# A two-layer hybrid decoder trunk: weight splits with priority, query stacks prepared earlier, selection rounds moved forward

## The chip, the cores and the metric

The kernel runs on one core of a Trainium2 chip. The core has five engines that run their own instruction queues side by side: TensorE (PE in the profile; PEld are its weight loads), VectorE (DVE), ScalarE (ACT), GpSimd (POOL) and SyncE (SP), which only issues DMAs here. The metric is the device time of one execution in microseconds; the runs of a kernel are summed up by their median.

## The reference, cut to what matters

A sequence of 512 tokens of width 1024 passes two layers. Each layer norms its input, projects it, and splits the columns among four attention groups of four heads each; their outputs are concatenated, projected and added, and a squared-ReLU MLP follows.

```
for l in range(2):
    h = rms_norm(x, norm1[l]);  proj = h @ w_in[l]            # 1024 -> 2764 columns
    # A: latent attention: q = rms_norm(a_cq) @ w_uq, k,v = rms_norm(a_ckv) @ w_ukv, rope on 32 of 96
    # B: sliding window of 128 keys, 2 key heads, a sink logit per head
    # C: score = sum_h w_h * relu(q_idx_h . k_idx); each query keeps its 128 best keys, attends over them
    # D: causal attention with a bias of cumulative log forget gates
    x = x + concat(o_a, o_b, o_c, o_d) @ w_out[l]
    x = x + square(relu(rms_norm(x, norm2[l]) @ w_up[l])) @ w_down[l]
out = rms_norm(x, final_norm)
```

All of it is float32.

## The kernel before

**Precision.** A float32 product is made of three matmuls (`mm3`, L126 to L129): each operand is split into a high part (a rounded copy, usually on ACT, L112) and a low part (what is left, a subtract, L122), and high by high, low by high and high by low are summed. So every weight tile of 128x1024 that is loaded (`raw`, three buffers, L206) goes through `split_weight` (L176): ACT writes `wh`, DVE or POOL writes `wl`. `weight` (L186) makes these splits one tile ahead of their use; letters in `PRM` (`wloi` to `wlop`) name the engine of each low part. The 16 tiles of `ww_d` in a layer hold the projection columns of groups B, C and D.

**Order.** PE's instructions stand as the code issues them. Those of the other engines are put in order by a scheduler at build time, which takes what it holds to be ready and, among these, what was issued first; `tc.high_priority(offset=HIGH)` moves what is issued under it ahead in that choice. Each engine then runs its list strictly as it stands and waits where an operand is not there.

**A layer's attention.** The projections are a `queue` of generators: `a` (32 steps of three matmuls, 416 columns), then `b0`, `b`, `d0`, `d`, `dv`, `c0`, `c`, `cv` (32 steps each, 256 columns), then the output projection's four parts. Wherever the code has work that leaves PE waiting, `fill(kind)` (L335) advances that queue by as many steps as a digit in `PLACES` says: `idx`, `qi` and `isc` in group C's indexer (`isc`: one digit for each of the 24 score products, L749), `aq` and `cq` around the transposes of the latent inputs (L816), `up` behind each tile of the latent query and key products, `a0` behind each step of the first pair's preparation.

Group A works on pairs of heads. `prep_a` turns its queries and keys by PE transposes (L491 in `parts`; L854 for the rotated 32 columns), splits them (`prt`, `kst`), and fills four stacks per pair by DMAs from SBUF to SBUF (`move`, L485, on SP's queue). The first pair's preparation is finished before the first unit.

**Units.** 64 units follow (head by query block of 128): 0 to 15 group A, 16 to 31 group B, 32 to 47 group D, 48 to 63 group C. A unit is a score on PE (L894 to L897 for A, L1003 to L1006 for B), a row maximum on DVE (`mn`, L541), the exponential on ACT (L544), the normalisation on POOL (L549), transposes on PE two units later (L555), their split, and the product with the values. `pace` puts projection steps between, so that PE gets 2600 ns of work per unit. The `softmax` and what follows on it is issued with high priority; the preparation of later families (`prep_b` and so on, with their `prt` splits and moves) and the selection are not.

**Selection.** Group C needs the 128 best of up to 512 keys per query: 16 rounds for each of three query blocks, each round a pair of DVE instructions (L770 finds the eight largest, L771 strikes them out). These 48 pairs are spread over the units by `extra` in `run_units`: `PRM["selr"]` gives the pairs per unit in units 0 to 15, 16 to 31, 32 to 47 and 48 to 63; at unit 45 all that are left are issued.

Of the kernel before, what the change touches and what calls it, by code (L numbers as in the profile page):

```python
# [16 lines left out]
P = 128  # L17
NL = 2
NT = 4
# [13 lines left out]
PLACES = {  # L33
    "idx": "k",
    "qi": "11111111",
    "isc": "111111111111111111111111",
    "cq": "444",
    "up": "22222222",
    "a0": "880",
    "aq": "606",  # L40
}

PRM = {
    "hold": ['g', 'b1'], "q3": "VGV", "high": 200, "gate_b": -1, "gate_d0": -1, "lag_b": 6, "lag_c": 4,
    "steps": 2, "pace": 2600, "quantum": 360, "burst": 5, "mlag": 4, "first": [0, 11, 18, 21, 26, 33, 41, 48], "psa": 2, "pss": 2, "pst": 3,
    "norm": "G", "vlo": "V", "wloi": "GVVV", "wloa": "VGGV",
    "wlo0": "GGVV", "wlo1": "GVGV", "wlop": "GGGG", "selr": [1.4, 1.0, 1.0, 1.2], "tlag": 2,
    "plag": 2, "rote": "VVGV", "rotp": "GVGGVGGGGVGVGGVG",
}

# [2 lines left out]
def tile_trunk(ctx: ExitStack, tc: tile.TileContext, x_d, consts_d, gains_d, sinks_d, fb_d, fin_d,  # L53
# [104 lines left out]
        return y  # L158


    wlist = []
    for L in range(NL):
        wlist += [(wi_d[L, kk], 600, WLI[kk], "y" if L and kk > 1 else "") for kk in range(4)]
        wlist += [(wa_d[L, kk], 832, WLA[kk], "") for kk in range(4)]
        wlist += [(ww_d[L, i, kk], 1024, (WL0 if i < 2 else WL1)[(2 * i + kk) % 4], "") for i in range(8) for kk in range(2)]
        for i in range(4):
            wlist += [(wo_d[L, i, :, 0:1024], 1024, WLP[i], ""), (wo_d[L, i, :, 1024:1536], 512, WLP[i], "")]
        wlist += [(wt_d[L, c], 1024, G, "") for c in range(2)]
        for half in range(2):
            wlist += [(wu_d[L, 16 * half + i], 1024, V, "") for i in range(16)]  # L170
            wlist += [(wd_d[L, half, c, fp], 1024, V, "x" if half and c and fp > 3 else "")
                      for c in range(2) for fp in range(8)]
    w_raw, w_split, w_at = [], [], [0]

    def split_weight(r, n, h, l, eng):
        hi(h, r[:, 0:n], S)  # L176
        lo(l, r[:, 0:n], h, eng)
# [7 lines left out]
    def weight(i, ahead=1):  # L185
        while len(w_raw) < min(len(wlist), i + 4) or len(w_split) < min(len(wlist), i + 1 + ahead):  # L186
            j = len(w_split)
            if j < min(len(w_raw), i + 1 + ahead):
                _, n, eng, where = wlist[j]
                p, c = (w_pools[where], 600 if where == "y" else 1024) if where else (whl, 1024)  # L190
                h = p.tile([P, c], F32R, tag="wh" + where, name="wh")
                l = p.tile([P, c], F32R, tag="wl" + where, name="wl")
                split_weight(w_raw[j], n, h[:, 0:n], l[:, 0:n], eng)
                w_split.append((h, l))
            else:
                load_weight()
        return w_split[i]
# [111 lines left out]
    for L in range(NL):  # L309
# [4 lines left out]
        with ExitStack() as ph:  # L314
# [17 lines left out]
            def ytile():  # L332
                return y_p.tile([P, NT, 256], F32, tag="y", name="y")
# [35 lines left out]
            def fill(kind):  # L369

                n = Q.get(kind, "")
                j = site.get(kind, 0)
                site[kind] = j + 1
                for _ in range(int(n[j], 36) if j < len(n) else 0):
                    if not queue or not advance():
                        break
# [435 lines left out]
            for j in range(3):  # L812
                fill("aq")
                ps = bank_b()
# [14 lines left out]
            hi(k2s[0][64:128, 0], ps[64:128], S)  # L829
            lo(k3s[64:96], ps[64:96], k2s[0][64:96, 0], V)  # L830
            ykn, ykv, yqn, yqr = (ytile() for _ in range(4))
            for t in range(NT):
                ps = bank("s")
                c = slice(t * P, (t + 1) * P)
                for j in range(2):
                    mm3(ps[:, 0:384], cth[j][:, c], ctl[j][:, c], wq_h[:, j * 384:(j + 1) * 384],
                        wq_l[:, j * 384:(j + 1) * 384], j == 0, j == 1)
                hi(yqr[:, t, 0:128], ps[:, 256:384], S, r2[:, t:t + 1])
                hi(yqn[:, t], ps[:, 0:256], S, r2[:, t:t + 1])
                rotate(yqr[:, t, 0:128], 4, 16, t, V)  # L840
                fill("up")
            for t in range(NT):
                ps = bank("s")
                c = slice(t * P, (t + 1) * P)
                mm3(ps, cth[2][:, c], ctl[2][:, c], wkv[:, 0], wkv[:, 1], True, True)
                hi(ykn[:, t], ps[:, 0:256], S, r2[:, 4 + t:5 + t])
                hi(ykv[:, t], ps[:, 256:512], S, r2[:, 4 + t:5 + t])
                fill("up")

            def prep_a(o, p):  # L850
                if p == 0:
                    ps = bank("t")
                    for t in range(NT):
                        T.transpose(ps[:, t * P:(t + 1) * P], yqr[:, t, 0:128], idf)  # L854
                    qrs.extend((kstack(), kstack()))
                    hi(qrs[0], ps, S)
                    lo(qrs[1], ps, qrs[0], V)
                if p:
                    k2s.append(stack())
                o["k1"], o["k2"], o["q1"], o["q2"] = stack(), k2s[p], stack(), stack()  # L860
                for h in range(2):
                    r = slice(64 * p + 32 * h, 64 * p + 32 * h + 32)
                    move(o["q2"][64:96, h], qrs[0][r])
                    move(o["q2"][96:128, h], qrs[1][r])
                for h in range(2):
                    if p or h:
                        move(o["k2"][64:128, h], k2s[0][64:128, 0])
                h_, l_ = parts(ykn, 128 * p)
                for h in range(2):
                    r = slice(64 * h, 64 * h + 64)  # L870
                    move(o["k1"][0:64, h], h_[r])
                    move(o["k1"][64:128, h], h_[r])
                    move(o["k2"][0:64, h], l_[r])
                yield
                h_, l_ = parts(yqn, 128 * p)
                for h in range(2):
                    r = slice(64 * h, 64 * h + 64)
                    move(o["q1"][0:64, h], h_[r])
                    move(o["q1"][64:128, h], l_[r])
                    move(o["q2"][0:64, h], h_[r])  # L880
                yield
                if p == 0:
                    o["vs"] = v_pair(heads(ykv, 0))
                    yield
# [2 lines left out]
                o["vs"] = v_pair(heads(ykv, P))  # L887
                yield

            qrs = []  # L890

            def score_a(o, ps, h, qb, n):
                c = slice(qb * P, (qb + 1) * P)
# [134 lines left out]
            units = []  # L1028
            os_ = {}
            for p in range(2):  # L1030
                o = os_["a", p] = {}
                preps.append((f"a{p}", FIRST[0], (), prep_a(o, p)))
                if p:
                    preps.append(("a1v", 8, (), prep_av(o)))
                units += causal_units(f"a{p}", score_a, o, p, lambda n: 3 * (n + 32) / 2.4 + 67)
# [301 lines left out]
```

## Time and profile before

| | |
|---|---|
| median of 3 runs | 1322.31 us (1321.92 to 1323.63) |
| the profiled execution | 1321.27 us, its span 1319.4 us |
| PE busy | 1257.7 us (95% of the span) |
| DVE busy | 758.3 us (57%) |
| ACT busy | 572.4 us (43%) |
| POOL busy | 260.3 us (20%) |
| mean granted clock of TensorE | 0.984 |

The span runs from the first to the last instruction of the profiled execution. Busy time of PE is time in which a matmul is in flight, at whatever clock; the granted clock is 1.00 at full speed (2.4 GHz) and 0.50 at half (1.2 GHz), so a window with a value between was at half speed for a part of it. The attention of the first layer takes the first 300 us or so of the span, its MLP the time to about 650 us, and the second layer repeats both.

### The profile page before, as it was taken

How to read it: one execution, taken by the hardware profiler on the slowest of the kernel's cores; microseconds unless marked ns; L12 is line 12 of the kernel's file. 1: busy time of each engine (PE TensorE's matmuls, PEld its weight loads, DVE VectorE, ACT ScalarE, POOL GpSimd, SP SyncE). 2: the span in 40 equal slices, each digit the busy share in tenths (PEclk: the TensorE clock that was granted, in tenths of full speed). 3: DMA queues.
4: the chain of work that ended last, by engine and by line, in shares of the span. 5: the costliest groups of instructions: out<-in, count | busy, mean ns of one | idle time of the engine just before them, and what ended most of it. 6: DMA issues, size and time to landing. Idle time of an engine off the chain costs nothing.

```text
span 1319.4 us, 19401 instructions
## 1 busy us (share of the span) xinstructions
PE 1257.7 (95%) x7232; PEld 1102.7 (84%) x7232; DVE 758.3 (57%) x1557; ACT 572.4 (43%) x1159; POOL 260.3 (20%) x356
## 2 busy tenths in 40 slices
PE   8798989999999999999998899899999999999997
PEld 7798878897888888888897889788988888888885
DVE  5677999845453334433366599997454523444344
ACT  5564555643442123323337455566344421233231
POOL 3353345441000000000033432454300000000011
PEclk9899989999999999999998999899999999999999
DMA  6126334523333333334411443453322333333331
GB/s 184 65 89 158 97 87 114 154 88 93 88 106 97 96 96 96 96 96 128 141 62 61 124 128 82 121 126 102 123 84 92 105 97 96 96 96 100 108 112 64
DMA packets 50818, 136.79 MB, mean 104 GB/s; under 512 B 7460, under 2 KB 7716, under 8 KB 50724
## 3 DMA queue, kind: packets, MB, share of 16 engines
q1 hardware_dynamic: 50724, 135.55, 35.6%
q8 instruction: 57, 0.93, 0.3%
q14 instruction: 37, 0.30, 0.1%
HBM read 106.95 MB, written 4.19 MB: 84 GB/s over the span
## 4 chain that ended last, share of the span: by engine, by line
PE 81%; DVE 13%; ACT 2%; DMA 1%; issue 1%; SPq 1%; POOL 1%; POOLq 0%; DVEq 0%; ACTq 0%
PE bank L129 24%; PE bank L127 24%; PE bank L128 24%; DVE isc L771 2%; DVE mn L541 2%; PE bank L555 2%; DVE m L770 2%; DVE pt1l L122 1%; DMA stk<-prt 1%; DVE wl L122 1%; PE bank L491 1%; PE bank L602 1%; PE bank L237 1%; ACT y L114 1%; PE bank L749 1%
## 5 line engine op out<-in xcount | busy, mean ns | idle before, releaser
L122 DVE TENSOR_TENSOR wl<-raw,wh 128x1024 fp32r<-128x1024 f32 (+2 forms) x154 | 186.5, 1213 | 229.7 <-ACT wh L112 229.0
L112 ACT ACTIVATE wh<-raw 128x1024 fp32r<-128x1024 f32 (+2 forms) x196 | 199.1, 1018 | 264.7 <-PE bank L128 229.2
L127 PE MATMUL bank<-wh,T 128*128 128x256 f32 (+3 forms) x864 | 272.5, 315 | 3.3 <-ACT T L241 1.8
L129 PE MATMUL bank<-wl,T 128*128 128x256 f32 (+3 forms) x864 | 257.5, 298 | 17.0 <-DVE wl L122 14.3
L128 PE MATMUL bank<-wh,T 128*128 128x256 f32 (+3 forms) x864 | 256.1, 296 | 0.2 <-DVE T L124 0.2
L129 PE MATMUL bank<-T,wh 128*128 128x512 f32 x512 | 199.5, 390 | 0.9 <-DVE T L124 0.9
L127 PE MATMUL bank<-T,wh 128*128 128x512 f32 x512 | 199.8, 390 | 0.0
L127 PE MATMUL bank<-wh,gh 128*128 128x512 f32 x512 | 199.6, 390 | 0.0
L128 PE MATMUL bank<-T,wl 128*128 128x512 f32 x512 | 199.5, 390 | 0.0
L129 PE MATMUL bank<-wl,gh 128*128 128x512 f32 x512 | 199.2, 389 | 0.0
L128 PE MATMUL bank<-wh,gl 128*128 128x512 f32 x512 | 199.2, 389 | 0.0
L129 PEld LDWEIGHTS bank<-wl,T 128*128 128x128 f32 x864 | 167.2, 194 | 20.8 <-DVE wl L122 15.2
L122 POOL TENSOR_TENSOR wl<-raw,wh 128x1024 fp32r<-128x1024 f32 (+3 forms) x42 | 91.8, 2185 | 420.7 <-DVE wl L122 336.5
L127 PEld LDWEIGHTS bank<-wh,T 128*128 128x128 f32 x864 | 168.5, 195 | 5.8 <-ACT T L241 2.2
L128 PEld LDWEIGHTS bank<-wh,T 128*128 128x128 f32 x864 | 167.9, 194 | 3.9 <-DVE T L124 0.5
L1134 DVE TENSOR_TENSOR a<-a 128x512 f32<-128x512 f32 x64 | 44.4, 693 | 154.1 <-ACT a L1133 154.1
L1133 ACT ACTIVATE a<-bank 128x512 f32<-128x512 f32 x64 | 38.3, 599 | 201.1 <-PE bank L129 201.1
L129 PEld LDWEIGHTS bank<-T,wh 128*128 128x128 f32 x512 | 96.1, 188 | 21.9 <-DVE T L124 1.8
L128 PEld LDWEIGHTS bank<-T,wl 128*128 128x128 f32 x512 | 96.1, 188 | 20.5 <-DVE wl L122 0.7
L127 PEld LDWEIGHTS bank<-T,wh 128*128 128x128 f32 x512 | 96.1, 188 | 19.9 <-ACT T L241 0.3
L129 PEld LDWEIGHTS bank<-wl,gh 128*128 128x128 f32 x512 | 96.1, 188 | 19.9
L127 PEld LDWEIGHTS bank<-wh,gh 128*128 128x128 f32 x512 | 96.1, 188 | 19.9
(223 smaller groups left out, 1847.0 us busy)
## 6 DMA issues: line engine op xcount, KB each, us to landing
raw<-in_wu_dram SPq DMA_DIRECT2D x64, 512.0 KB, 3.6
raw<-in_wd_dram SPq DMA_DIRECT2D x64, 512.0 KB, 3.6
stk<-prt SPq DMA_DIRECT2D x144, 128.0 KB, 2.4
raw<-in_ww_dram SPq DMA_DIRECT2D x32, 512.0 KB, 3.5
T<-in_x_dram SPq DMA_DIRECT2D x16, 256.0 KB, 4.2
raw<-in_wo_dram SPq DMA_DIRECT2D x8, 512.0 KB, 3.7
raw<-in_wa_dram SPq DMA_DIRECT2D x8, 416.0 KB, 3.2
raw<-in_wi_dram SPq DMA_DIRECT2D x8, 300.0 KB, 3.5
```

The source lines that it names most:

```text
L112: S.activation(out=out, in_=in_, func=AF.Copy)
L114: S.activation(out=out, in_=in_, func=AF.Copy, scale=scale)
L122: eng.tensor_tensor(out=out, in0=in_, in1=f(h), op=OP.subtract)
L127: T.matmul(out, ah, bh, start=start, stop=False)
L128: T.matmul(out, al, bh, start=False, stop=False)
L129: T.matmul(out, ah, bl, start=False, stop=stop)
L541: red[0] = V.tensor_reduce(out=mn, in_=ps[:, 0:nv], axis=AX.X, op=OP.max, negate=True)
L555: T.transpose(ps[:, b * P:(b + 1) * P], pr[:, b * P:(b + 1) * P], idf)
L770: V.max(out=m8, in_=sc)
L771: V.match_replace(out=sc, in_to_replace=m8, in_values=sc, imm_value=GONE)
L1133: S.activation(out=a, in_=ps, func=AF.Relu)
L1134: V.tensor_tensor(out=a, in0=a, in1=a, op=OP.mult)
```

## The change

Four things change; none adds or removes an instruction.

- The splits of the 16 `ww_d` tiles of each layer are issued with `HIGH` priority (`w_hot`).
- The first pair's preparation is taken apart into `q_part` and `k_part`. `q_part` of the first pair is issued inside the loop over the latent keys' tiles, behind its second tile, with two projection steps; `k_part` stays where `prep_a` was. In the second pair the query half now comes first too.
- `PLACES` moves projection steps: 36 instead of 24 go among the indexer's score products, 6 instead of 12 each to `aq` and `cq`, 18 instead of 16 to `up`.
- `selr` issues 1.8 selection pairs per unit instead of 1.4 in units 0 to 15, 0.8 instead of 1.0 and 0.9 instead of 1.0 in the next two groups. `mlag` 3 instead of 4 lets an output step use a finished head one unit sooner.

```diff
-    "isc": "111111111111111111111111",
-    "cq": "444",
-    "up": "22222222",
-    "a0": "880",
-    "aq": "606",
+    "isc": "121212121212121212121212",
+    "cq": "222",
+    "up": "222222222",
+    "a0": "88",
+    "aq": "303",
...
-    "steps": 2, "pace": 2600, "quantum": 360, "burst": 5, "mlag": 4, "first": [0, 11, 18, 21, 26, 33, 41, 48], "psa": 2, "pss": 2, "pst": 3,
+    "steps": 2, "pace": 2600, "quantum": 360, "burst": 5, "mlag": 3, "first": [0, 11, 18, 21, 26, 33, 41, 48], "psa": 2, "pss": 2, "pst": 3,
...
-    "wlo0": "GGVV", "wlo1": "GVGV", "wlop": "GGGG", "selr": [1.4, 1.0, 1.0, 1.2], "tlag": 2,
+    "wlo0": "GGVV", "wlo1": "GVGV", "wlop": "GGGG", "selr": [1.8, 0.8, 0.9, 1.2], "tlag": 2,
...
-    wlist = []
+    wlist, w_hot = [], []
     for L in range(NL):
...
         wlist += [(wa_d[L, kk], 832, WLA[kk], "") for kk in range(4)]
+        w_hot += range(len(wlist), len(wlist) + 16)
...
-                split_weight(w_raw[j], n, h[:, 0:n], l[:, 0:n], eng)
+                with tc.high_priority(offset=HIGH if j in w_hot else 0):
+                    split_weight(w_raw[j], n, h[:, 0:n], l[:, 0:n], eng)
...
+            qrs, os_a = [], ({}, {})
+
+            def q_part(o, p):
+
+                if p == 0:
+                    ps = bank("t")
+                    for t in range(NT):
+                        T.transpose(ps[:, t * P:(t + 1) * P], yqr[:, t, 0:128], idf)
+                    qrs.extend((kstack(), kstack()))
+                    hi(qrs[0], ps, S)
+                    lo(qrs[1], ps, qrs[0], V)
+                o["q1"], o["q2"] = stack(), stack()
+                h_, l_ = parts(yqn, 128 * p)
+                for h in range(2):
+                    r = slice(64 * p + 32 * h, 64 * p + 32 * h + 32)
+                    move(o["q2"][64:96, h], qrs[0][r])
+                    move(o["q2"][96:128, h], qrs[1][r])
+                    r = slice(64 * h, 64 * h + 64)
+                    move(o["q1"][0:64, h], h_[r])
+                    move(o["q1"][64:128, h], l_[r])
+                    move(o["q2"][0:64, h], h_[r])
+
+            def k_part(o, p):
+
+                if p:
+                    k2s.append(stack())
+                o["k1"], o["k2"] = stack(), k2s[p]
+                h_, l_ = parts(ykn, 128 * p)
+                for h in range(2):
+                    r = slice(64 * h, 64 * h + 64)
+                    move(o["k1"][0:64, h], h_[r])
+                    move(o["k1"][64:128, h], h_[r])
+                    move(o["k2"][0:64, h], l_[r])
+                    if p or h:
+                        move(o["k2"][64:128, h], k2s[0][64:128, 0])
...
                 hi(ykv[:, t], ps[:, 256:512], S, r2[:, 4 + t:5 + t])
                 fill("up")
+                if t == 1:
+                    q_part(os_a[0], 0)
+                    fill("up")
...
             def prep_a(o, p):
-                if p == 0:
...
                 if p:
+                    q_part(o, p)
+                    yield
+                k_part(o, p)
                 yield
```

Three places show what becomes of the order; line numbers of the changed kernel are two higher in its upper part (L541 and L543 are the same maximum). The first is SP's queue ahead of the first unit: `kst` and `prt` are the split queries and keys, `raw` is a weight load. Before:

```order
L206 DMA raw<-in_ww_dram 128x1024 x2
L485 DMA stk<-stk 64x512
L206 DMA raw<-in_ww_dram 128x1024
L485 DMA stk<-kst 32x512 x4
L485 DMA stk<-prt 64x512 x12
L485 DMA stk<-kst 32x512 x4
L485 DMA stk<-stk 64x512 x2
```

Of the change:

```order
L208 DMA raw<-in_ww_dram 128x1024
L487 DMA stk<-kst 32x512 x2
L487 DMA stk<-prt 64x512 x3
L487 DMA stk<-kst 32x512 x2
L487 DMA stk<-prt 64x512 x9
L208 DMA raw<-in_ww_dram 128x1024
L487 DMA stk<-kst 32x512 x2
```

The ten moves of the queries come first now, then the keys' six, and a weight load has moved ahead of the second pair's moves.

The second is DVE ahead of unit 16, the first of group B: `prt` are the low parts of that group's keys and queries (the second one, the queries), `mn` the units' row maxima, MAX and MATCH_REPLACE the selection. Before, units 13 to 15:

```order
L541 TENSOR_REDUCE mn<-bank 128x1
L122 TENSOR_TENSOR prt<-bank,prt 128x512
L116 CAST stk<-yst 128x8x64
L122 TENSOR_TENSOR prt<-bank,prt 128x512
L545 RECIPROCAL sm<-sm 128x1
L122 TENSOR_TENSOR pt1l_393<-bank,pt1h_389 128x4x128
L541 TENSOR_REDUCE mn<-bank 128x1
L122 TENSOR_TENSOR pt0l_400<-bank,pt0h_396 128x128
L122 TENSOR_TENSOR stk<-yst,stk 128x8x64
L541 TENSOR_REDUCE mn<-bank 128x1
```

Of the change, from behind unit 15's maximum to unit 16's:

```order
L773 MATCH_REPLACE isc<-m_1861,isc 128x384
L772 MAX m_1864<-isc 128x8
L122 TENSOR_TENSOR prt<-bank,prt 128x512
L773 MATCH_REPLACE isc<-m_1864,isc 128x512
L772 MAX m_1904<-isc 128x8
L772 MAX m_1907<-isc 128x8
L773 MATCH_REPLACE isc<-m_1904,isc 128x256
L773 MATCH_REPLACE isc<-m_1907,isc 128x384
L772 MAX m_1951<-isc 128x8
L772 MAX m_1954<-isc 128x8
L773 MATCH_REPLACE isc<-m_1951,isc 128x512
L543 TENSOR_REDUCE mn<-bank 128x1
```

The queries' low part has moved from behind unit 13's maximum to behind unit 15's, and eight selection instructions stand between it and unit 16's.

The third is PE among the indexer's score products (L749, L751 in the change), with projection steps of `a` (416 columns) and `b0` (256) between. Before:

```order
L749 MATMUL bank<-kst,stk 128x384
L127 MATMUL bank<-wh,T 128x256
L128 MATMUL bank<-wh,T 128x256
L129 MATMUL bank<-wl,T 128x256
L749 MATMUL bank<-kst,stk 128x512
```

Of the change:

```order
L751 MATMUL bank<-kst,stk 128x256
L127 MATMUL bank<-wh,T 128x256
L128 MATMUL bank<-wh,T 128x256
L129 MATMUL bank<-wl,T 128x256
L127 MATMUL bank<-wh,T 128x256
L128 MATMUL bank<-wh,T 128x256
L129 MATMUL bank<-wl,T 128x256
L751 MATMUL bank<-kst,stk 128x384
```

Every second product has two steps behind it instead of one.

## Rows read from the trace of the kernel before

**Rows 1.** The page, section 1: busy us, share, instructions by engine.

```profile
PE 1257.7 (95%) x7232; PEld 1102.7 (84%) x7232; DVE 758.3 (57%) x1557; ACT 572.4 (43%) x1159; POOL 260.3 (20%) x356
```

**Rows 2.** Waits of PE: for whom, us in total, times, longest.

```profile
PE bank L129 <- DVE wl L122: 14.3, 4, 6.0
PE bank L749 <- DVE isc L756: 8.2, 6, 2.3
PE bank L894 <- DMA stk<-prt: 7.1, 2, 3.6
...
PE bank L749 <- DVE isc L754: 2.3, 2, 1.1
```

**Rows 3.** Windows: busy us (instructions) of PE, PEld, DVE, ACT, POOL; clock, DMA, GB/s.

```profile
50.00:60.00 10.00, 4.79 (x23) 3.75 (x22) 6.99 (x16) 7.51 (x26) 5.38 (x14) 0.74 0.07 22
60.00:70.00 10.00, 10.00 (x60) 9.68 (x59) 7.42 (x14) 6.84 (x15) 0.00 (x0) 0.75 0.09 36
100.00:110.00 10.00, 6.13 (x38) 5.71 (x37) 1.49 (x7) 2.71 (x5) 3.44 (x6) 0.83 0.75 168
130.00:140.00 10.00, 9.46 (x77) 8.68 (x76) 10.00 (x26) 5.48 (x16) 4.94 (x5) 1.00 0.18 52
170.00:180.00 10.00, 4.77 (x41) 4.47 (x39) 10.00 (x22) 4.29 (x11) 3.71 (x5) 0.88 0.02 5
```

**Rows 4.** Timeline of PE and SP, and the chain, ahead of unit 0.

```profile
87.44 0.39 PE L127 MATMUL bank<-stk,T 128*128 128x512 f32 x1
88.85 0.40 PE L127 MATMUL bank<-stk,T 128*128 128x512 f32 x1
97.39 7.60 SPq L485 DMA_DIRECT2D stk<-prt  x12
102.47 2.34 DMA stk<-prt
104.27 0.36 PE L894 MATMUL bank<-stk 128*128 128x256 f32 x1 [3.55 <-DMA stk<-prt]
```

**Rows 5.** Timeline, last indexer update to first latent query product.

```profile
72.37 0.74 DVE L756 SCALAR_TENSOR_TENSOR isc<-bank,wf,isc 128x512 f32<-128x512 f32 x1
75.31 0.33 SPq L805 DMA_DIRECT2D raw<-in_uq_dram  x1
79.13 1.21 DVE L122 TENSOR_TENSOR stk<-raw,stk 128x768 fp32r<-128x768 f32 x1 [0.73 <-ACT stk L112]
80.32 0.42 PE L127 MATMUL bank<-stk,T 128*128 128x384 f32 x1
```

**Rows 6.** Timeline of DVE and PE: maxima of units 0, 16, 48, a `prt`, a split.

```profile
105.59 0.29 DVE L541 TENSOR_REDUCE mn<-bank 128x1 f32<-128x128 f32 x1 [5.32 <-PE bank L897]
143.68 0.68 DVE L122 TENSOR_TENSOR prt<-bank,prt 128x512 fp32r<-128x512 f32 x1
150.48 0.29 DVE L541 TENSOR_REDUCE mn<-bank 128x1 f32<-128x130 f32 x1 [0.49 <-PE bank L1006]
180.72 0.58 PE L129 MATMUL bank<-wl,T 128*128 128x256 f32 x1 [5.95 <-DVE wl L122]
244.76 0.29 DVE L541 TENSOR_REDUCE mn<-bank 128x1 f32<-128x128 f32 x1 [0.56 <-PE bank L907]
```

**Rows 7.** Groups of DVE instructions, 105 to 150 us: busy us, mean ns.

```profile
L771 DVE MATCH_REPLACE8 isc<-m,isc 128x256 f32<-128x256 f32 (+2 forms) x18 | 9.7, 543 | 0.0
L770 DVE MAX8 m<-isc 128x8 f32<-128x256 f32 (+2 forms) x18 | 9.4, 547 | 0.0
...
L771 DVE MATCH_VALUE_LOAD isc<-m,isc 128x8 f32 x18 | 1.4, 80 | 0.0
...
L122 DVE TENSOR_TENSOR wl<-raw,wh 128x1024 fp32r<-128x1024 f32 x1 | 1.2, 1206 | 0.0
```

**Rows 8.** Timeline of DVE and POOL near 56 us.

```profile
56.00 2.33 DVE L155 TENSOR_TENSOR u<-y 128x8 f32<-128x8 f32 x1
55.97 2.35 POOL L122 TENSOR_TENSOR wl<-raw,wh 128x1024 fp32r<-128x1024 f32 x1 [0.54 <-ACT wh L112]
```

More of the change, by code (lines that the diff above doesn't have):

```diff
@@ L848, in tile_trunk @@
                 fill("up")
+                if t == 1:
+                    q_part(os_a[0], 0)
+                    fill("up")
             def prep_a(o, p):
-                if p == 0:
[L852 to L857, printed above, removed]
-                if p:
[L859 to L880, printed above, removed]
+                if p:
+                    q_part(o, p)
+                    yield
+                k_part(o, p)
                 yield
@@ L888, in prep_av @@
                 yield
-            qrs = []
             def score_a(o, ps, h, qb, n):
@@ L1030, in tile_trunk @@
             for p in range(2):
-                o = os_["a", p] = {}
+                o = os_["a", p] = os_a[p]
                 preps.append((f"a{p}", FIRST[0], (), prep_a(o, p)))
```

## The prediction, made before the change ran

> **What bounds the kernel now.** I read the page's first section first: TensorE (PE) is busy for 1257.7 of the 1319.4 us of the span, VectorE (DVE) for 758.3 [rows 1]. The change alters no work: the built orders of before and after hold the same instructions on every engine, so a gain can only come out of PE's 61.7 idle us and of the stretches in which its clock is low. Next come PE's waits by cause [rows 2]. The longest are two, one per layer, of 6.0 us for a weight split on DVE, and two of 3.55 us for the moves that fill the first pair's stacks; eight more, 10.5 us in all, are waits of the indexer's products for DVE. The windows then show that each place also costs clock [rows 3]: half speed for a part of 50 to 70 us (0.74 and 0.75, so 10 x 0.26 + 10 x 0.25 = 5.1 us lost), of 100 to 110 (0.83: 1.7 us) and of 170 to 180 (0.88: 1.2 us). The same windows show DVE busy for 10.00 of 10 us at 130 and at 170. So in the attention units DVE is as much the bound as PE; ahead of them it has room.
>
> All durations below are from the first layer; the second repeats the program, and I take it at the same price. I count per layer and double.
>
> **Part 1, the latent queries' stacks (L831 to L894).** Ahead of the first unit SyncE (SP) issues 4 moves from `kst` and 12 from `prt`, these in 7.60 us, 0.63 each. The last one that the first score needs is issued at 102.47 and takes 2.34 us to land; PE, idle since 100.7, starts its score at 104.27 after 3.55 us [rows 4]. In the new order the query half is issued first, and its transposes stand two tiles of the latent keys' loop earlier on PE. Such a tile takes 88.85 - 87.44 = 1.41 us [rows 4], so the chain on SP, still 16 moves long, begins up to 2.8 us sooner, and the wait shrinks by 2.8. The two extra projection steps that stand there now (less than a tile's 1.41 us) hide most of what is left. The low clock behind the wait costs 1.7; I take half of that back, 0.9, since a wait of some tenths may remain. Gain 3.7. Bounds: 0, if the transposes wait for the queries' rotation on DVE, which has to come first; and 5.2, if wait and low clock both go.
>
> **Part 2, the indexer's products (`isc`, `cq`, `aq`).** The 24 products now have 36 projection steps between them instead of 24; the 12 come out of `aq` and `cq`, so that up to the first latent query product it is 76 steps either way. PE's waits there are 5.2 us a layer [rows 2] and the low clock costs 5.1, but that is not the gain. The first query product starts at 80.32 [rows 5], and what it needs is a chain: the last score update on DVE (ends 72.37 + 0.74 = 73.1), the load of `uq`, issued at 75.31, and its split on DVE, which starts at 79.13 and ends at 80.34. In the new order DVE does one weight split and one rotation more inside the stage and so ends it no sooner than 73.1; behind it come the mask cast and then the load, at the soonest 73.7. Load to end of split takes 80.34 - 75.31 = 5.0 us: the split ends at 78.7, and 12 steps of cover stand ahead of its reader where 24 stood. Gain 80.3 - 78.7 = 1.6, or 2.4 where the load doesn't wait for the cast; I take 2.0. Bounds: 0 (the cover being too thin) and 5.2, the waits themselves.
>
> **Part 3, splits with priority and earlier selection rounds, taken together because both reorder DVE.** Before, DVE runs the gate's arithmetic ahead of the split for which PE waits 5.95 us, until 180.72 [rows 6]. In the new order that split stands several units earlier: this wait goes, and with it the 1.2 us of clock. But DVE is full there, so the work has only changed places. Up to unit 16 DVE runs 18 selection pairs now [rows 7]; counted in the new order 24 and a half stand ahead of that unit's maximum. A pair costs 0.547 + 0.543 + 0.080 = 1.17 us [rows 7], so 6.5 pairs are 7.6 us, and one weight split more (1.21 [rows 7]) stands there too: 8.8 us on an engine without gaps. Moreover the window group's query parts, which have no priority, are pushed back: before, the second `prt` subtract ran at 143.68, 6.8 us ahead of unit 16's maximum at 150.48 [rows 6]; now it stands behind unit 15's maximum with only eight selection instructions (4 x 0.547 + 4 x 0.543 = 4.4 us) between. Two moves (1.3 us) and a landing (2.34) follow on it, 3.6 us, which those eight fill. PE will wait for unit 16.
>
> From unit 0's maximum to unit 16's it is now 150.48 - 105.59 = 44.9 us, and from there to unit 48's 244.76 - 150.48 = 94.3 [rows 6]. I take the first as 6.5 longer: 8.8, less some two us in which DVE waits now behind unit 0 while PE is slow (100 to 110: DVE 1.49 busy, clock 0.83 [rows 3]). The second has 8.8 us less for DVE to do and 5.95 + 1.2 = 7.2 us less of PE's waiting and lost clock; I take 7.5 shorter. Gain 1.0. Bounds: a loss of 4.6 (8.8 later, a low clock of 1.7 as behind the other wait, only 5.95 back) and a gain of 3.8 (5 later, all 8.8 back).
>
> A rule speaks against the change here. The Trainium skill ("PSUM — Partial Sum Buffer", "Engine vs sequencer instructions") says that VectorE's queue is strictly first in, first out. By that every round placed ahead of unit 16's maximum delays it in full; the sum this gives is rival 5.
>
> The rest I cost at nothing: `mlag` 3 and the steps that leave the tail change only where projection steps stand in the last units. Behind the last head 8 of them are left of 13, at some 0.4 us each (two, with three longer products, make a tile of 1.41): 3.2 us over the head's four evictions, at some 0.6 each (512 columns, half a split's 1.21).
>
> **Sum.** 3.7 + 2.0 + 1.0 = 6.7 per layer, 13.4 in all. The profiled execution took 1321.3 us, 1.0 below the median of the runs; 1321.3 - 13.4 + 1.0 gives **1309 us**, its own range 1304 to 1314.
>
> **Rivals.**
> 1. *Slower: preparation starves behind selection.* Only splits got priority; the `prt` parts of later families queue behind the rounds as at unit 16. That one family is in the sum. For each further one (units 24, 32, 40) PE waits 3.6 us and loses 1.7 of clock, 5.3. Against it: from unit 24 on fewer rounds are left. With the full loss of 4.6 at unit 16 and one more family, a layer gains 3.7 + 2.0 and loses 9.9: 8.4 in all, **1331**. It decides once a second family is late.
> 2. *The first stacks come no sooner*, part 1 being held by the rotation or by SP's queue. For it: SP's moves are as many as before. Gain 2 x 3.0: **1316**.
> 3. *New collisions of DVE with GpSimd (POOL).* A DVE operation on 128x8 elements took 2.33 us, ending at 58.33 as POOL's split of 2.35 us did at 58.32 [rows 8]. Two more such blocks per layer, 2.2 each, on a full DVE cost 8.8: **1318**. The order can't tell which will coincide. The Trainium skill ("SBUF — State Buffer", "Who interferes with whom") says that a DVE operation with two SBUF inputs and a GpSimd one that reads SBUF lock each other out for a whole instruction; the trace agrees with it in that pair.
> 4. *All waits go.* 5.2 + 3.0 + 3.8 = 12 per layer, the bounds of parts 1 and 3 with most of part 2's: **1298**. Against it: DVE's windows at 10.00.
> 5. *Unit 16 is late in full.* 8.8 later and 7.5 back, a loss of 1.3 instead of a gain of 1.0, so 3.7 + 2.0 - 1.3 = 4.4 a layer: **1313.5**. Against it: DVE's idle time behind unit 0. This is the strict queue of the page named in part 3.
>
> **Chances.** Forecast 0.38, starving 0.14, no sooner 0.14, collisions 0.12, all 0.14, late in full 0.08. A measurement of this kernel tells 0.2% from no change, 1319.7 to 1325.0. Faster: 0.38 + 0.08 + 0.11 + 0.07 + 0.14 = 0.78 (of rivals 2 and 3 a part falls within the 0.2%); same 0.08; slower 0.14. The range that leaves out the slower case and little else is 1298 to 1321.
>
> **What would show it.** Part 1: the first `L894` score of a layer waits under 1.5 us, and the window around it has a granted clock near 1.00. Part 2: the first latent query product starts 1.5 to 2.5 us earlier, with the waits for `isc` halved. Part 3: no wait of 6 us for a split; unit 16's maximum about 6.5 us later behind unit 0's, with a new PE wait for moves just ahead of it, and unit 48's at 138 instead of 139.2 us behind unit 0's. The forecast is wrong if waits for `prt` moves stand ahead of units 24, 32 or 40 too, if the 3.55 us stay, or if DVE's mean durations grow.

## The result and the profile after

The changed kernel takes **1311.97 us** (median of 4 runs, 1310.78 to 1312.30) against 1322.64 us before on the same chip: ratio **0.9917, 95% interval 0.9900 to 0.9934**. The forecast was 1309, with 1298 to 1321 around it. The profiled execution took 1312.3 us, its span is 1310.5 us.

PE's waits by cause in the changed kernel (us in total, times, the longest):

```profile
PE bank L1017 <- DMA stk<-prt: 11.1, 2, 5.6
PE bank L751 <- DVE isc L756: 4.8, 2, 2.4
...
PE bank L602 <- DVE tmp L572: 4.4, 2, 2.2
...
PE bank L129 <- DVE stk L122: 2.4, 1, 2.4
PE bank L908 <- DMA stk<-prt: 1.6, 1, 1.6
PE bank L751 <- DVE isc L758: 1.6, 2, 0.8
```

Against [rows 2]: the splits' 14.3 us are gone, the first scores' 7.1 us have become 1.6, all of it in the second layer (and 0.5 for the matmul behind), the indexer's 10.5 have become 6.4. New are 5.6 us per layer at `L1017`, unit 16's score, 2.2 per layer at `L602`, the last matmuls of a head, and 2.4 in the first layer at a product with the latent query weights' low part.

Windows of the changed kernel, four of the stretches of [rows 3] and three more (after the length: busy us of PE, PEld, DVE, ACT, POOL, then PE's clock, DMA share, GB/s):

```profile
50.00:60.00 10.00, 6.82 (x38) 6.26 (x37) 4.56 (x11) 8.33 (x27) 5.59 (x16) 0.81 0.22 77
60.00:70.00 10.00, 10.00 (x68) 9.69 (x67) 7.87 (x15) 6.88 (x15) 0.88 (x2) 0.85 0.08 21
...
100.00:110.00 10.00, 9.63 (x78) 9.05 (x77) 5.70 (x17) 3.90 (x11) 6.24 (x10) 1.00 0.84 206
140.00:150.00 10.00, 5.13 (x39) 4.64 (x39) 9.84 (x26) 2.98 (x8) 1.74 (x3) 0.92 0.40 108
150.00:160.00 10.00, 8.74 (x60) 8.55 (x61) 9.63 (x36) 3.69 (x10) 3.25 (x3) 0.74 0.12 26
170.00:180.00 10.00, 10.00 (x87) 9.83 (x86) 9.85 (x28) 6.50 (x17) 4.54 (x4) 1.00 0.17 55
210.00:220.00 10.00, 7.80 (x51) 7.21 (x50) 7.17 (x19) 5.05 (x14) 2.64 (x6) 0.83 0.44 112
```

The holes at 100 and 170 are closed, at full clock. A new hole stands at 140 to 160, with DVE busy for 9.84 and 9.63 of 10 us: PE is waiting for an engine that does not rest. Another stands at 210.

The timeline around unit 16 (start, duration, engine, operation; in brackets PE's idle time and what ended it):

```profile
148.10 0.67 DVE L122 TENSOR_TENSOR prt<-bank,prt 128x512 fp32r<-128x512 f32 x1
...
151.26 0.55 PE L1017 MATMUL bank<-stk 128*128 128x256 f32 x1 [5.62 <-DMA stk<-prt]
...
152.64 0.28 DVE L543 TENSOR_REDUCE mn<-bank 128x1 f32<-128x130 f32 x1
```

The queries' low part ends 2.5 us ahead of the score and starts 4.5 us ahead of unit 16's maximum; before, it started 6.8 us ahead of that maximum [rows 6]. Between the two DVE does the eight selection instructions that the order showed.

The same execution of the first layer in stretches: from the first latent query product to unit 0's maximum, from there to unit 16's, and from there to unit 48's. Where later only two rows stand, they are the last two. Before:

```profile
80.32:105.59 25.27, 21.18 (x153) 20.07 (x152) 13.67 (x30) 12.59 (x27) 12.56 (x19) 1.00 0.51 138
105.59:150.48 44.89, 43.25 (x334) 40.36 (x333) 40.72 (x112) 26.50 (x66) 14.25 (x19) 0.96 0.50 127
150.48:244.76 94.28, 85.51 (x692) 81.90 (x692) 91.21 (x241) 55.87 (x144) 43.55 (x57) 0.96 0.44 115
```

After:

```profile
78.67:103.81 25.14, 22.16 (x156) 20.74 (x157) 14.48 (x33) 12.58 (x27) 10.29 (x16) 1.00 0.52 136
103.81:152.64 48.83, 42.36 (x335) 39.51 (x334) 47.00 (x134) 25.87 (x66) 13.82 (x19) 0.96 0.49 128
152.64:240.91 88.27, 85.54 (x691) 82.64 (x690) 78.99 (x222) 56.47 (x145) 42.33 (x58) 0.97 0.45 117
```

From unit 0 to unit 16 DVE has 6.3 us more to do, and the stretch is 3.9 us longer; the next one is 6.0 us shorter. Unit 48 comes 137.1 us behind unit 0, 139.2 before. The second layer's two rows take 44.0 and 93.9 us before and 48.8 and 88.5 after. Odd is the first row: it is as long as before, although the first score's wait is gone. The experiments come back to it.

### The profile page after: what moved, and what is told of

The parts are those of the page before. It is cut to its first block, busy times and chain, and to the rows that moved or that the text cites. A ratio compares the mean times of both kernels' runs of the same rounds, so it can differ in the third digit from the quotient of the medians.

```text
span 1310.5 us, 19442 instructions
## 1 busy us (share of the span) xinstructions
PE 1258.5 (96%) x7232; PEld 1104.4 (84%) x7232; DVE 745.1 (57%) x1557; ACT 570.9 (44%) x1159; POOL 254.1 (19%) x356
## 5 line engine op out<-in xcount | busy, mean ns | idle before, releaser
L122 POOL TENSOR_TENSOR wl<-raw,wh 128x1024 fp32r<-128x1024 f32 (+3 forms) x42 | 88.6, 2109 | 409.9 <-DVE wl L122 336.4
L128 PEld LDWEIGHTS bank<-wh,gl 128*128 128x128 f32 x512 | 96.1, 188 | 19.9
```

Source lines behind the costliest of these rows:

```text
L122: eng.tensor_tensor(out=out, in0=in_, in1=f(h), op=OP.subtract)
L128: T.matmul(out, al, bh, start=False, stop=False)
```

## Experiments

Each kernel was timed in 5 rounds against the kernel before; medians of the latter lay between 1322.3 and 1323.6 us, so a difference between kernels that were not timed together is good to about 1 us. "Query half" is the new preparation order with the steps of `up` and `a0` that belong to it, "steps" the digits of `isc`, `cq` and `aq`, "splits" the priority, "rates" `selr`.

### One part alone

**Splits.** On the kernel before:

```diff
-                split_weight(w_raw[j], n, h[:, 0:n], l[:, 0:n], eng)
+                with tc.high_priority(offset=HIGH if j in w_hot else 0):
+                    split_weight(w_raw[j], n, h[:, 0:n], l[:, 0:n], eng)
```

> The kernel before with the splits' priority alone. Theory 'waits': the 6 us wait for a split and the low clock behind it (1.2 us) go in each layer, and nothing else comes later, since in the built order unit 16's preparation keeps its place: 1322.6 - 2 x 7.2 = 1308 us, between 1306 and 1312; unit 16's maximum at most 1.2 us later behind unit 0's, unit 48's about 132 us behind it. Rival 'DVE is full': the work only changes places on a full engine, other waits take the place of the one removed, unit 48's maximum stays 138 to 139 us behind unit 0's and the time at 1320 to 1323 us.

1315.87 us, ratio 0.9952 (0.9939 to 0.9964): between the two. The 6 us wait is gone, but unit 48's maximum is still 137.7 us behind unit 0's, and PE waits for moves ahead of unit 32 in its place (2.0 and 2.2 us). So in the units DVE was nearly full, as the rival says. Part of the gain lies elsewhere, in the indexer: from its first to its last score product (before, then with the splits' priority)

```profile
47.00:69.45 22.45, 17.25 (x93) 15.85 (x93) 14.80 (x29) 16.34 (x48) 6.61 (x19) 0.77 0.15 47
```

```profile
48.28:68.66 20.38, 16.52 (x94) 15.47 (x93) 12.07 (x25) 16.32 (x48) 6.48 (x19) 0.83 0.15 52
```

it is 2.1 us shorter, and 2.0 in the second layer: DVE has 2.7 us less to do inside it, and PE's last wait there (2.27 us) is gone. The indexer's waits are 6.5 us in all here, so what the whole change has left of them (6.4) is reached without the steps.

**Rates.** On the kernel before:

```diff
-"selr": [1.4, 1.0, 1.0, 1.2]
+"selr": [1.8, 0.8, 0.9, 1.2]
```

> The kernel before with the new selection rates alone. Theory 'selection delays unit 16': the wait of about 5.5 us ahead of unit 16's score is there as in the changed kernel, with 2 to 3 us of low clock behind it, and unit 16's maximum 4 us or more later behind unit 0's; the tenth weight split stands ahead of unit 16 in this order too, so that the 6 us wait should be gone as well, which leaves 1322 to 1328 us. Rival 'the splits' priority delays unit 16': no wait of over 1 us there, and 1308 to 1318 us, since the 6 us wait goes and nothing comes instead.

1320.37 us, ratio 0.9984 (0.9974 to 0.9993). A wait of 5.4 us at unit 16 is there without any priority, so the rates cause it; the 6 us wait is gone too, as the built order had it. A small gain remains, better than the range expected.

**Query half.** The change with the other edits undone:

```diff
-    "isc": "121212121212121212121212",
-    "cq": "222",
-    "aq": "303",
+    "isc": "111111111111111111111111",
+    "cq": "444",
+    "aq": "606",
-"mlag": 3, "selr": [1.8, 0.8, 0.9, 1.2]
+"mlag": 4, "selr": [1.4, 1.0, 1.0, 1.2]
-                with tc.high_priority(offset=HIGH if j in w_hot else 0):
+                with tc.high_priority(offset=HIGH if j in () else 0):
```

> The changed kernel with the old steps in the indexer, the old selection rates, mlag 4 and no priority for splits: what is left is the query half issued ahead, with the steps that go with it. Theory 'the first score's wait is worth its time': the 3.55 us wait goes in each layer with the 1.7 us of low clock, 3.7 to 5.2 us a layer, so 1312 to 1315 us; and since in this order the tenth split has come to stand ahead of unit 16 by itself, up to 7.2 us a layer more, down to 1298 us. Rival 'DVE gives it back': unit 0 comes 4 us earlier and unit 48 does not, 1320 to 1323 us.

1311.33 us, ratio 0.9919 (0.9904 to 0.9933): this one edit gives as much as the whole change. Its stretches, as above:

```profile
81.21:103.72 22.51, 21.89 (x159) 20.79 (x157) 13.59 (x29) 12.58 (x27) 12.38 (x19) 1.00 0.58 154
103.72:145.73 42.01, 42.01 (x342) 39.70 (x341) 40.15 (x115) 26.45 (x67) 15.40 (x19) 1.00 0.53 136
145.73:239.05 93.32, 85.35 (x685) 82.05 (x684) 88.55 (x241) 55.91 (x145) 40.98 (x58) 0.96 0.45 117
```

The first score waits 0.3 us at most; PE is busy for all of the 42.01 us from unit 0 to unit 16, at full clock. The split's wait is not removed; it has moved to just ahead of unit 32:

```profile
193.10 0.58 PE L129 MATMUL bank<-wl,T 128*128 128x256 f32 x1 [5.69 <-DVE wl L122]
```

**Steps.** On the kernel before:

```diff
-    "isc": "111111111111111111111111",
-    "cq": "444",
-    "aq": "606",
+    "isc": "121212121212121212121212",
+    "cq": "222",
+    "aq": "303",
```

> The kernel before with the new steps among the indexer's products alone (isc, cq, aq). Theory 'steps are worth 2.0 a layer' (the prediction's part 2): 1322.3 - 4 = 1318 us. Rival 'steps only move the wait': the scores' waits fall, but the latent query weights' low part is late by 2 us or more in the first layer, and the moves of the first stacks are waited for as before: 1321 to 1326 us.

1322.30 us, ratio 0.9990 (0.9982 to 0.9999): about 1.3 us in all, where part 2 had 4. The rival holds, though its new wait for the low part is only 0.8 us here.

**Splits and rates together**, both edits above on the kernel before:

```diff
-"selr": [1.4, 1.0, 1.0, 1.2]
+"selr": [1.8, 0.8, 0.9, 1.2]
...
+                with tc.high_priority(offset=HIGH if j in w_hot else 0):
```

> The kernel before with the splits' priority and the new selection rates, without the query half and the steps. The prediction's part 3 gives 1.0 a layer, 1322.3 - 2 = 1320 us, with a wait of 5 us or more ahead of unit 16. Theory 'the rates cost what they cost in the changed kernel': 1315.9 + 5.1 = 1321 us. Rival 'they add up as each did alone' (splits 6.5 us, rates 2.0 us): 1314 us.

1314.05 us, ratio 0.9927 (0.9913 to 0.9940): they add up. Unit 16 now waits 7.5 us, and still the sum gains:

```profile
103.65:154.94 51.29, 43.57 (x334) 40.59 (x334) 47.48 (x136) 26.21 (x66) 13.80 (x19) 0.93 0.46 121
154.94:239.33 84.39, 84.15 (x692) 81.42 (x691) 77.32 (x219) 55.18 (x144) 42.21 (x57) 0.98 0.47 123
```

With the splits alone the two took 44.18 and 93.51 us: 7.1 are lost and 9.1 come back.

### Parts taken out of the changed kernel

**Old rates.**

```diff
-"selr": [1.8, 0.8, 0.9, 1.2]
+"selr": [1.4, 1.0, 1.0, 1.2]
```

> The changed kernel with the old selection rates. Theory 'moving rounds forward cost time': the 5.5 us wait ahead of unit 16 and the 2 to 3 us of low clock around it go in each layer and little comes back, since DVE has idle time behind unit 32: 1312.0 - 2 x (4 to 8) = 1296 to 1304 us. Rival 'DVE is full up to unit 48': the 6.5 pairs (7.6 us) that go back behind unit 16 are paid there, unit 48's maximum stays about 137 us behind unit 0's, and the time is 1310 to 1314 us.

1306.88 us, ratio 0.9884 (0.9870 to 0.9897), 5 us faster than the whole change and between what the theory and the rival had.

```profile
103.62:145.88 42.26, 42.26 (x342) 39.76 (x341) 40.17 (x114) 26.46 (x67) 15.37 (x19) 1.00 0.55 148
145.88:237.53 91.65, 84.52 (x684) 80.82 (x683) 87.34 (x241) 56.26 (x144) 39.96 (x58) 0.98 0.44 113
```

With the query half, units 0 to 15 are bound by PE (42.26 of 42.26 us busy) with DVE just below it (40.17). The rates put 6.8 us more on DVE there, and the stretch grows by 6.6; behind it only 3.4 us come back. In the second layer the kernel with the old rates has a low clock (the last section shows it), and the rates cost 4.7 us and give 4.4 back. With the old steps in both kernels they cost 6.6 and 7.9 us in the two layers and give 3.8 and 4.7 back.

**Old steps.**

```diff
-    "isc": "121212121212121212121212",
-    "cq": "222",
-    "aq": "303",
+    "isc": "111111111111111111111111",
+    "cq": "444",
+    "aq": "606",
```

> The changed kernel with the old steps among the indexer's products, the new selection rates kept. Theory 'the steps' loss is paid ahead of unit 0 and stays': 1312.0 - 4.3 = 1307 to 1308.5 us, unit 16's maximum still 48.8 us behind unit 0's. Rival 'what is late at unit 16 swallows it': 1310.5 to 1312.5 us, unit 16 later behind unit 0 by as much as unit 0 is earlier.

1308.94 us, ratio 0.9885 (0.9872 to 0.9899). This is half a microsecond above what the first theory had. The steps' loss is paid ahead of unit 0 of the first layer and stays; there unit 16's maximum comes 48.8 us behind unit 0's with the steps and without. Nor do the steps bring the first latent query product forward. With them:

```profile
78.67 0.44 PE L127 MATMUL bank<-stk,T 128*128 128x384 f32 x1 [0.36 <-ACT stk L112]
```

Without:

```profile
78.89 0.42 PE L127 MATMUL bank<-stk,T 128*128 128x384 f32 x1
```

Either way that is 31.1 us behind the indexer's first score product; before it was 33.3, with the splits' priority alone 31.2, with the steps alone 32.8.

**Old rates and old steps**, both edits above together:

```diff
-    "isc": "121212121212121212121212",
-    "cq": "222",
-    "aq": "303",
+    "isc": "111111111111111111111111",
+    "cq": "444",
+    "aq": "606",
-"selr": [1.8, 0.8, 0.9, 1.2]
+"selr": [1.4, 1.0, 1.0, 1.2]
```

> The changed kernel with the old selection rates and the old steps among the indexer's products; against the kernel with the old selection rates alone (1306.9 us) it tells what the new steps are worth. Theory 'steps are worth 2.0 a layer' (the prediction's part 2): 1306.9 + 4.0 = 1311 us, its first latent query product 2 us later. Rival 'nothing gained': the waits for the indexer's scores fall by about 2 us a layer, and the first layer waits 2.3 us at the low part of the latent query weights instead; 1306 to 1308 us. With splits' priority here and none in the kernel with the query half alone (1311.3 us), 1309 to 1311 us is also what that part would give without the steps.

**1302.57 us, ratio 0.9845 (0.9830 to 0.9859)**, outside what either theory had: the steps don't gain, they cost 4.3 us here. No kernel of the study is faster. It keeps the query half, the splits' priority and `mlag` 3:

```profile
78.85:101.33 22.48, 21.89 (x159) 20.79 (x158) 14.68 (x31) 12.56 (x27) 12.51 (x19) 1.00 0.58 157
101.33:143.60 42.27, 42.27 (x341) 39.65 (x340) 40.19 (x115) 26.33 (x67) 15.32 (x19) 1.00 0.57 148
143.60:235.22 91.62, 84.56 (x686) 80.97 (x685) 87.33 (x240) 56.27 (x145) 39.80 (x58) 0.98 0.44 113
```

### Where the steps' gain went, and what holds unit 16

**Mask constants elsewhere.** On the kernel with the old rates (and the new steps):

```diff
-                mk = raw_p.tile([P, 1024], F32, tag="raw", name="mk")
+                mk = temp()
```

> The changed kernel with the old selection rates, and with the mask constants of the first layer loaded into a temporary tile instead of a weight-load buffer. Theory 'the load of the latent query weights waits for a buffer': that load no longer stands behind one more weight split, its low part comes ahead of the mask cast on DVE, and the 2.3 us wait in the first layer goes, the second layer staying as it is: 1306.9 - 2 to 2.8 = 1304 to 1305 us. Rival 'the split's place on DVE decides, behind the rotation and the norm's arithmetic': the wait stays over 1.5 us and the time within 1 us of 1306.9.

1303.16 us, ratio 0.9851 (0.9836 to 0.9865): 3.7 us less, somewhat more than expected, and not to be told from the fastest. The wait went, and with it the low clock behind it (0.94 over 26.7 us before the edit, 1.00 after). That makes unit 0 of the first layer 2.1 us earlier. The rest of the gain lies in the second layer, although the edited line runs in the first alone: there the first score waits 0.74 us instead of 1.40, and units 0 to 15 run at a clock of 1.00 instead of 0.96. Why was not settled. In the changed kernel the timeline shows the cause of the wait:

```profile
73.29 1.25 DVE L122 TENSOR_TENSOR wl<-raw,wh 128x1024 fp32r<-128x1024 f32 x1 [0.18 <-ACT wh L112]
...
74.57 0.33 SPq L807 DMA_DIRECT2D raw<-in_uq_dram  x1
...
77.78 0.83 ACT L112 ACTIVATE stk<-raw 128x768 fp32r<-128x768 f32 x1
...
79.34 0.20 DVE L157 SCALAR_TENSOR_TENSOR y<-u,y 128x8 f32<-128x8 f32 x1
79.46 0.74 DVE L124 SCALAR_TENSOR_TENSOR T<-bank,gains,T 128x512 fp32r<-128x512 f32 x1
80.13 1.50 DVE L122 TENSOR_TENSOR stk<-raw,stk 128x768 fp32r<-128x768 f32 x1
...
81.68 0.44 PE L129 MATMUL bank<-stk,T 128*128 128x384 f32 x1 [2.39 <-DVE stk L122]
```

The load of `uq` is issued as a weight split ends and frees its buffer, 0.7 us earlier than before [rows 5]. Its high part is done on ACT at 78.6, but DVE has the last step of the norm and the transposed inputs' low part ahead in its order, so the low part runs at 80.13 instead of 79.13, and PE, which has fewer steps left as cover, waits until 81.68 for a matmul that before ran at 80.76. With the constants elsewhere the load is free one split sooner and the low part runs at 74.85.

**Preparation at high priority**, on the changed kernel and on the one with the old rates:

```diff
-                hi(h_, ps, S)
-                lo(l_, ps, h_, V)
+                with tc.high_priority(offset=HIGH):
+                    hi(h_, ps, S)
+                    lo(l_, ps, h_, V)
```

> The changed kernel with the preparation's splits at high priority and nothing else. Theory 'unit 16 waits because its queries' low part stands behind the selection': that part now stands ahead of unit 14's maximum, the 5.5 us wait goes, with the low clock behind it: 1312.0 - 2 x (5.5 to 8) = 1296 to 1301 us if DVE's rounds ahead of unit 16 (22 pairs where 25 stood) cost nothing by themselves; 1302 to 1307 us if their time (4 pairs more than with the old rates, 4.7 us a layer) is still paid at unit 16. Rival 'the wait is for DMA, not for DVE's order': the wait stays at 5 us or more, 1310 to 1314 us.

1307.07 us, ratio 0.9885 (0.9865 to 0.9904). In the first layer unit 16's score waits 0.9 us instead of 5.6 (1.8 in the second), so the place of the preparation on DVE did make that wait; unit 16 comes 45.8 us behind unit 0, 3.6 more than with the old rates. The wait is shortened, the rounds' time is still paid.

> The changed kernel with the old selection rates, and with the preparation's splits (high and low part) issued at high priority. Theory 'preparation must stand ahead of selection': the waits for moves ahead of units 16 and 32 that are left with the old rates (1 to 3 us at each, with some low clock) go: 1306.9 - 2 x (1 to 3) = 1301 to 1305 us. Rival 'DVE is full': what the preparation gains, the probabilities' low parts (pt1l) lose, which PE waits for too; 1305.5 to 1310 us.

1306.85 us, ratio 0.9877 (0.9862 to 0.9892), no gain over the old rates alone. The rival holds: the waits for moves shrink, and PE waits for probabilities instead (2.33 us for `pt1l` at 241.66).

**Group D's preparation one unit earlier**, on the fastest kernel (old rates and old steps):

```diff
-"first": [0, 11, 18, 21, 26, 33, 41, 48]
+"first": [0, 11, 18, 21, 25, 33, 41, 48]
```

> The changed kernel with the old selection rates and the old steps, and with the preparation of the third family (group D) released one unit earlier (25 instead of 26). Theory 'preparation released too late': the 2 us wait for moves ahead of unit 32 goes in both layers, with the low clock of the second: 1302.6 - 2 x (1.5 to 2.5) = 1297.5 to 1299.5 us. Rival 'DVE is full up to unit 48': three rounds that stood ahead of unit 32 now stand behind it (33 pairs ahead where 36 were) and delay what follows; unit 48's maximum stays 133 to 135 us behind unit 0's and the time at 1301.5 to 1304 us.

1309.69 us, ratio 0.9897 (0.9882 to 0.9911): 7 us slower than without it, and slower than either theory had. Unit 32 comes 5.2 us earlier in the first layer (87.0 us behind unit 0 instead of 92.2), and then the second pair of group D is late (at `issue` the profile shows nothing that PE waited for):

```profile
213.81 0.35 PE L978 MATMUL bank<-stk 128*128 128x256 f32 x1 [2.30 <-issue]
216.42 0.55 PE L980 MATMUL bank<-gk,stk 128*128 128x256 f32 x1 [2.19 <-DMA stk<-kst]
```

Unit 48 ends 138.8 us behind unit 0 instead of 133.9. The high part of that pair's keys ends on ACT at 191.9, and the low part runs on DVE at 209.55, with nine selection instructions in between; without the edit it runs at 199.22. That is the prediction's first rival, starving preparation, made by a step that looked like a cure.

## Why the prediction was right, and where its sum was not

The direction, the range and the places held; the sum of 6.7 per layer was measured as 5.3, made of parts that were mis-sized in both directions. Timed apart, the query half, the steps, and the splits with the rates gain 11.0, 1.3 and 9.6 us, 21.9 together; in one kernel they give 10.7. That the total came near the forecast is errors that cancel, and so luck. Of the signs, two were missed: the first score of the second layer still waits 1.64 us, where 1.5 was the bound, and the waits for `isc` fell by four tenths, not by half.

**Part 1, 3.7 per layer: right in mechanism, too small.** Alone the query half is worth 11.0 us, 5.5 per layer, above the upper bound of 5.2. The wait went as worked out. The step that failed is "I take half of that back" for the low clock: all of it came back, and so did the waits inside units 0 to 15, which had no term (PE idle for 1.6 us there before, for none with the query half). The traces show one thing that went with them. Before, a subtract on DVE takes 2.58 us while POOL makes a weight split (130.03 to 132.44):

```profile
130.41 2.58 DVE L122 TENSOR_TENSOR stk<-y,stk 128x512 fp32r<-128x512 f32 x1
```

In every kernel with the query half or the new rates it takes 0.66 to 0.79 us. What this is worth by itself was not measured.

**Part 2, 2.0 per layer: wrong.** The first latent query product does start 1.65 us earlier (78.67), near the forecast, but not by the steps: without them it starts at 78.89. The step that failed is the chain behind it: load to end of split was taken over at 5.0 us. It became 7.1 in the first layer (74.57 to 81.63), because the split stands behind the norm's arithmetic on DVE. The bound had named the case ("the cover being too thin") at 0 instead of at a loss. In the changed kernel the steps cost 3.0 us, of which 2.4 by unit 0 of the first layer. With the old rates they cost 4.3, of which 2.3 by there; the rest lies in the second layer, whose units 0 to 15 run at a clock of 0.96 with the steps and 1.00 without, and why is open. Alone the steps gain 1.3.

**Part 3, 1.0 per layer: the mechanism right, its sizes not.** Splits and rates alone gain 4.8 us per layer, above the upper bound of 3.8. Unit 16 was to come 6.5 us later, from 8.8 us more work for DVE less some 2 of its idle time, and came 3.9 later. The idle time fell by 2.3 us as worked out; mis-sized was the 8.8, which measured 6.3. Six more rounds and a split stand there as counted, but their durations were added up although they overlap (a strike of 0.67 us at 148.76 is followed by the next instruction at 149.35), and the subtract of 2.58 us has become 0.79. That unit 16 comes 6.6 us later than in the kernel with the old rates is another comparison, and near 6.5 by chance. The 1.2 us of clock behind the split's wait were misread too: in the window from 170 to 180 PE stood idle from 174.8 on and lost nothing; the half clock that it paid for stands behind the wait, 0.50 from 180.7 to 184.0.

Two terms were missing. The splits' priority also shortens the indexer's stage by 2.1 us. And the rates' sign goes with the query half: some 2 us gained without it, 5 lost with it (`mlag` differs between these kernels as well). With it, the rounds moved forward push units 0 to 15 over PE's own 42.3 us, and of what they cost only 3.4 us come back, because the stretch behind unit 16 has a wait of 2.2 us (1.6 with the old rates) and the low clock behind it (0.83), where the kernel with splits and rates alone ran 84.4 us without one:

```profile
211.13 0.59 ACT L571 ACTIVATE tmp<-bank 64x512 f32<-64x512 f32 x1 [3.62 <-POOL y L472]
...
211.76 0.68 DVE L572 TENSOR_TENSOR tmp<-bank,tmp 64x512 f32<-64x512 f32 x1 [2.06 <-ACT tmp L571]
...
212.59 0.35 PE L602 MATMUL bank<-pt0h,stk 128*128 128x256 f32 x1 [2.20 <-DVE tmp L572]
```

Read upwards: PE waits for a head's sum on DVE, that for a copy on ACT, and that for a rotation on POOL. Why the kernel without the query half has no such wait was not settled.

**At nothing: `mlag`.** From unit 63's maximum to the first matmul of the MLP that needs a low part it takes 32.3 us in the kernel with the query half alone (274.92 to 307.24) and 30.9 in the fastest (270.14 to 301.01). All kernels with `mlag` 3 show the shorter time, all with 4 the longer, in both layers: some 1.4 us per layer that the sum had at nothing. Each of the other edits stands alone in a kernel with the longer time, but `mlag` was not run alone, so that it is the cause follows by elimination and is not shown directly.

**Rivals.** Starving preparation did not come in this kernel but in another. The strict order (rival 5; the Trainium skill, "PSUM — Partial Sum Buffer", "Engine vs sequencer instructions") is borne out where DVE has no idle time: 6.8 us more work ahead of unit 16's maximum made it 6.6 us later. Its time of 1313.5 us is nearer to the result than the forecast's 1309, but by chance, since its terms (8.8 us later, 7.5 back) measured 3.9 and 6.0 against the kernel before. New collisions did not decide: DVE is busy for 745.1 us, 758.3 before [rows 1].

## What to carry to other kernels

Take parts of a change apart before adding them up: steps and rates cost 9 us together here, hidden behind a query half that gained 11 alone and a splits' priority that gained 6.5 alone. A sign that comes true does not show its cause: the query product came earlier by about the amount forecast, but not through the edit that was to bring it. Work moved ahead on a full engine was paid in full where it was put and given back only as far as the next bound, so compare the busy time of both engines in the stretch that receives it, without the waits that other edits remove. When a load is moved or covered differently, follow it past its landing to the place of its first user in that engine's order.

## What the runs showed of the hardware

Waits of like length did not cost the same clock. With the old rates the first score of the second layer (at 742.19) waits 1.40 us, and the clock is 0.62 and 0.53 in the 4 us behind it, so mostly at 1.2 GHz; in the changed kernel it waits 1.64 us (until 746.91) and the clock stays 1.00. In both PE had been busy for 4 us without a gap shortly before (735 to 739 and 740 to 744):

```profile
743.00:745.00 2.00, 2.00 (x12) 1.97 (x12) 1.18 (x5) 0.99 (x3) 0.20 (x1) 0.62 0.88 239
745.00:747.00 2.00, 2.00 (x12) 2.00 (x11) 0.00 (x0) 0.76 (x2) 1.57 (x2) 0.53 0.59 215
```

```profile
747.00:749.00 2.00, 1.72 (x13) 1.52 (x14) 0.79 (x4) 0.49 (x3) 0.00 (x0) 1.00 1.01 215
749.00:751.00 2.00, 2.00 (x19) 1.96 (x19) 0.71 (x3) 1.86 (x3) 1.38 (x2) 1.00 0.86 300
```

And the rival of collisions is real as a mechanism: in the fastest kernel a rotation's product of 128x128 on DVE takes 2.41 us (the next one of this shape, at 189.56, takes 0.28) while POOL makes a weight split:

```profile
186.82 2.41 DVE L467 TENSOR_TENSOR tmp<-y,rope 128x128 f32<-128x128 f32 x1
```

```profile
186.75 2.34 POOL L122 TENSOR_TENSOR wl<-raw,wh 128x1024 fp32r<-128x1024 f32 x1 [0.61 <-ACT wh L112]
```

Everything behind it on DVE comes 2 us later; how much of that PE pays was not measured. The pair agrees with the rule of the Trainium skill ("SBUF — State Buffer", "Who interferes with whom") that the third rival named.
